# Moving the pads around h: the split activations 128 bytes instead of 64 off the weights' place in a 256-byte line

## The chip, the cores and the metric

The kernel runs on one core of a Trainium2 chip. The metric is the device time in microseconds (us), the median of the runs; lower is better. The core has TensorE (PE, matmuls; its weight loads are shown apart as PEld), VectorE (DVE), ScalarE (ACT), GpSimd (POOL), and SyncE (SP), which here only issues transfers (DMA).

## The reference

Two transformer blocks after one another, on 256 tokens of 1,024 values, all in float32. What is matrix work, in order (normalizations, modulation and residuals between them left out):

```python
# first block, layer 0
y = gmlp(h)                        # h @ w_in (1024 x 4096), spatial mix, @ w_out
x = x + g2 * moe(h)                # 64 experts, 8 for each token, 1 shared
# first block, layer 1
y = moba_attention(h)              # k, v, q, o projections of 1024 x 1024
x = x + g2 * moe(h)
# second block, layers l = 0 and 1
x = x + 0.5 * (silu(h @ Wg) * (h @ Wu)) @ Wd      # "ffn1": 1024 -> 2 x 2816 -> 1024
x = x + hybrid(h)                                 # h @ w_in (1024 x 5120), small mixes, @ w_out
x = x + 0.5 * (silu(h @ Wg) * (h @ Wu)) @ Wd      # "ffn2"
```

In each line `h` is the normalized `x`, newly made.

## The kernel before, in words

Tokens lie along the free dimension: `x` is a tile of 128 partitions by 8 groups of 256 tokens. The normalized activation is kept as two tiles of the same shape, `hH` (rounded to float32r) and `hL` (what the rounding left), and each weight in the same way as `WH` and `WL`. A product is then three matmuls, the function `mm3` at line 290: `WH` with `hH`, `WH` with `hL`, `WL` with `hH`. All go through `mm` at line 287, so the profile puts nearly every matmul down to L288.

Weights come in pieces of 1 MB (128 partitions by 2,048 float32) into a ring of nine slots, issued by SP. ACT rounds each piece into `WH` (L243), DVE makes `WL` (L246); there are two such pairs of buffers, so that a piece is split while another is used. A piece is an item; the items' order is written out by hand, and `run` at line 210 goes through it. The kinds of item that matter here:

- `proj_b` (line 381), the upward products of gmlp's second half, attention, hybrid and the feed-forward parts: weights from `WH`/`WL` stationary, 256 columns of `hH` or `hL` moving, 48 matmuls for each piece. `proj_a` (line 389) is the same with the sides changed: 128 columns of `hH` or `hL` stationary, 256 columns of `WH` or `WL` moving.
- `down_d` (line 396), the downward products: weights from `WH`/`WL` stationary, hidden values moving, which lie in the tile `rarena`; 48 matmuls for each piece. A feed-forward part is 22 upward and 11 downward items, mixed: two up, one down.
- `shared_mm` (line 1039), the shared expert: two of its upward steps take the stationary weights from `rarena` and move `hH` or `hL`.

At the start of each part of the second block the row of normalizers is made on TensorE: squares are summed (`stat_mm`, line 336), and two transposes (`stat_row`, L356, operands `cst` and `nv`) come between the third and the fourth item. The first of the feed-forward parts does this otherwise (`first_rows`, line 1534).

The tiles are laid out in a partition in the order of their declaration, each size rounded up to a multiple of 32 bytes. `WH`, `WL`, `x`, `hH`, `hL` are 16,384, 16,384, 8,192, 8,192 and 8,192 bytes, all multiples of 256, so that two tiles with no pad between them stand at the same place of a 256-byte line. With `pad0` of 64 bytes `hH` and `hL` stand 64 bytes behind the place of `WH` and `WL` in the line. With `pad1`, and the tiles after it, `rarena` too stands 64 bytes behind (it begins 107,584 bytes after `WH`, which is 420 lines and 64 bytes). All slices that matmuls take of these tiles are at multiples of 256 bytes from the tile's start, but for the scatter's and gather's small ones.

Of the kernel before, what the change touches and what calls it, by code (L numbers as in the profile page):

```python
# [8 lines left out]
F32 = mybir.dt.float32  # L9
# [85 lines left out]
def moba_moe_hybrid_kernel(ctx: ExitStack, tc: tile.TileContext, A: dict):  # L95
# [6 lines left out]
    def sb(shape, dt, name):  # L102
        return pool.tile(shape, dt, name=name)
# [5 lines left out]
    WL = sb([128, 4, 1024], F32R, "WL")  # L109
    x = sb([128, KD, T], F32, "x")  # L110

    sb([128, 16], F32, "pad0")
    hH = sb([128, KD, T], F32R, "hH")
    hL = sb([128, KD, T], F32R, "hL")
    sb([128, 16], F32, "pad1")
    cols = sb([128, NCOL], F32, "cols")
    cst = sb([128, NCST], F32, "cst")
    mbias = sb([128, 128], F32, "mbias")
# [1783 lines left out]
```

## Time and profile before

| | |
|---|---|
| time, median of 3 runs | 2583.36 us (2569.75, 2583.36, 2583.38) |
| profiled execution: time, span | 2581.31 us, 2579.3 us |
| PE, PEld | 95%, 73% of the span busy, 17,938 instructions each |
| DVE, ACT, POOL | 53%, 40%, 0% |
| DMA | 724 MB, mean 281 GB/s |
| granted TensorE clock, mean | 0.984 of full speed |

A matmul's record overlaps with the next one's: its busy time says when TensorE has something in it, not how fast it goes. The pace is the step from the start of one matmul to the start of the next.

### The profile page before, as it was taken

The numbers are of one execution on the slowest core, as the hardware profiler recorded it, in microseconds if no ns is written. First come the engines' busy times: TensorE is split into PE (matmuls) and PEld (weight loads), VectorE is DVE, ScalarE is ACT, GpSimd is POOL, SyncE is SP. The second block draws the span as 40 slices with busy tenths as digits, with TensorE's granted clock in tenths as the row PEclk, the third lists the DMA queues.
The fourth block names the chain that finished last, engine by engine and source line by source line (L and its number), as shares of the span: only waits on it lengthen the run. The fifth ranks groups of instructions, "written<-read, shape, count | busy, mean of one in ns | idle before, by whom it ended". The sixth has DMA issues, their size and how long they took to land. (4 is left out here: it accounts for less than half of the span.)

```text
span 2579.3 us, 43882 instructions
## 1 busy us (share of the span) xinstructions
PE 2437.8 (95%) x17938; PEld 1894.9 (73%) x17938; DVE 1359.6 (53%) x2536; ACT 1042.5 (40%) x1710; POOL 3.8 (0%) x6
## 2 busy tenths in 40 slices
PE   6998899999989979999999899999999999999998
PEld 4885554444448845544444699999999999999998
DVE  4556232332347643323233665788665666887665
ACT  3333222222225532212222444576544544684543
POOL 0000000000000000000000000000000000000000
PEclk9998999999999989999999899999999999999999
DMA  9878899999966389999999454354655553454750
GB/s 389 318 270 326 334 414 421 421 421 420 421 284 251 158 320 365 405 421 421 420 421 421 181 196 180 123 186 175 246 196 196 191 192 143 171 180 156 270 196 17
DMA packets 101437, 724.45 MB, mean 281 GB/s; under 512 B 11248, under 2 KB 12528, under 8 KB 14192
## 3 DMA queue, kind: packets, MB, share of 16 engines
q1 hardware_dynamic: 100080, 718.32, 70.7%
q8 instruction: 143, 2.34, 0.4%
q10 hardware_dynamic: 1152, 3.28, 0.3%
q14 instruction: 62, 0.51, 0.1%
HBM read 720.50 MB, written 1.05 MB: 280 GB/s over the span
## 5 line engine op out<-in xcount | busy, mean ns | idle before, releaser
L288 PE MATMUL pb<-rarena,WH 128*128 128x256 f32 x3552 | 701.5, 284 | 34.2 <-DVE farena L1207 22.0
L243 ACT CAST WH<-ring 128x1024 fp32r<-128x1024 f32 x476 | 489.4, 1047 | 434.2 <-PE pb L288 348.6
L288 PE MATMUL pb<-hH,WH 128*128 128x256 f32 x2336 | 654.1, 280 | 3.3 <-ACT hH L1505 2.4
L288 PE MATMUL pb<-hH,WL 128*128 128x256 f32 x2336 | 651.2, 279 | 2.5 <-DVE WL L246 2.4
L288 PE MATMUL pb<-hL,WH 128*128 128x256 f32 x2336 | 650.8, 279 | 0.0
L246 DVE TENSOR_TENSOR WL<-ring,WH 128x1024 fp32r<-128x1024 f32 x476 | 570.8, 1215 | 147.8 <-ACT WH L243 145.1
L288 PEld LDWEIGHTS pb<-rarena,WH 128*128 128x128 f32 x3552 | 577.0, 189 | 51.7 <-ACT farena L1110 28.2
L288 PE MATMUL pb<-rarena,WL 128*128 128x256 f32 x2224 | 591.8, 281 | 3.8 <-DVE WL L246 2.3
L288 PE MATMUL pb<-ring,farena 128*32 128x512 f32 (+2 forms) x2064 | 434.7, 595 | 23.4 <-DMA ring<-ex 23.4
L288 PEld LDWEIGHTS pb<-hH,WH 128*128 128x128 f32 x2336 | 440.1, 188 | 15.6 <-ACT WH L243 7.1
L288 PEld LDWEIGHTS pb<-hH,WL 128*128 128x128 f32 x2336 | 439.8, 188 | 3.9 <-DVE WL L246 3.7
L288 PEld LDWEIGHTS pb<-hL,WH 128*128 128x128 f32 x2336 | 440.0, 188 | 0.2 <-DVE hL L1502 0.2
L288 PEld LDWEIGHTS pb<-rarena,WL 128*128 128x128 f32 x2224 | 421.5, 190 | 5.7 <-DVE WL L246 3.0
L288 PEld LDWEIGHTS pb<-ring,farena 128*32 128x32 f32 (+2 forms) x2064 | 136.1, 130 | 239.9 <-issue 188.7
L1147 DVE SCALAR_TENSOR_TENSOR tmp<-pb,small,tmp 128x256 f32<-128x256 f32 x56 | 27.1, 484 | 413.0 <-ACT tmp L1145 413.0
L288 PE MATMUL pb<-ring,tmp 128*32 128x512 f32 (+2 forms) x1024 | 228.1, 605 | 16.8 <-DMA ring<-ex 8.6
L288 PEld LDWEIGHTS pb<-ring,tmp 128*32 128x32 f32 (+2 forms) x1024 | 70.0, 131 | 169.7 <-issue 145.7
L1180 DVE TENSOR_TENSOR WL<-pb,WH 128x512 fp32r<-128x512 f32 x112 | 77.5, 692 | 183.9 <-ACT WH L1179 183.9
L1207 DVE TENSOR_TENSOR farena<-farena,pb 128x512 f32<-128x512 f32 x208 | 133.6, 684 | 60.2 <-PE pb L288 60.2
L831 DVE TENSOR_TENSOR tmp<-pb,R 128x512 f32<-128x512 f32 x88 | 60.8, 691 | 184.8 <-PE pb L288 181.1
L1179 ACT CAST WH<-pb 128x512 fp32r<-128x512 f32 x112 | 65.7, 587 | 190.6 <-PE pb L288 190.6
L1161 ACT COPY tmp<-pb 128x256 f32<-128x256 f32 x56 | 20.9, 372 | 287.7 <-PE pb L1159 287.7
(301 smaller groups left out, 1710.6 us busy)
## 6 DMA issues: line engine op xcount, KB each, us to landing
ring<-ex SPq DMA_DIRECT2D x384, 1024.0 KB, 12.7
ring<-ada SPq DMA_DIRECT2D x56, 1024.0 KB, 8.3
ring<-f1u SPq DMA_DIRECT2D x44, 1024.0 KB, 4.8
ring<-f2u SPq DMA_DIRECT2D x44, 1024.0 KB, 4.9
ring<-win SPq DMA_DIRECT2D x40, 1024.0 KB, 4.8
ring<-f1d SPq DMA_DIRECT2D x22, 1024.0 KB, 4.8
ring<-f2d SPq DMA_DIRECT2D x22, 1024.0 KB, 4.8
ring<-lu SPq DMA_DIRECT2D x10, 1024.0 KB, 4.8
```

Source lines behind the costliest of these rows:

```text
L243: S.copy(hi, raw)
L246: V.tensor_sub(lo, raw, hi)
L288: P.matmul(out, l, r, start=start, stop=stop, skip_group_check=True, **kw)
L831: V.tensor_tensor(t.rearrange("p (a t) -> p a t", a=2), hold["p"].rearrange("p (a t) -> p a t", a=2), R.rearrange("p (o t) -> p o t", o=1) ...
L1147: V.scalar_tensor_tensor(hh, bank[:, 256:], wsl[:, b % 2:b % 2 + 1], t[:, :256], op0=ALU.mult, op1=ALU.mult)
L1161: S.copy(t, bank[:, :256])
L1179: S.copy(yH[:, fs], PB[DN[f]])
L1180: V.tensor_tensor(yL[:, fs], PB[DN[f]], yH[:, fs], op=ALU.subtract)
L1207: V.tensor_tensor(a2, a2, bank, op=ALU.add)
```

## The change

One pad of 128 bytes stands before `hH`, and none behind `hL`:

```diff
-    sb([128, 16], F32, "pad0")
+    sb([128, 32], F32, "pad0")
     hH = sb([128, KD, T], F32R, "hH")
     hL = sb([128, KD, T], F32R, "hL")
-    sb([128, 16], F32, "pad1")
     cols = sb([128, NCOL], F32, "cols")
```

`hH` and `hL` move up by 64 bytes; no other tile moves, since the two pads together were 128 bytes too. Against `WH` and `WL` they now stand 128 bytes off in the 256-byte line, against `rarena` 64 bytes (on the other side of the line's start), where they stood 64 and 0. No instruction is added, removed or moved.

## Rows read from the trace of the kernel before

**Rows 1.** Busy time by stage (--windows): length, engines' busy us (instructions), granted clock, DMA share, GB/s
```profile
0.00:160.00 160.00, 138.50 (x1082) 109.57 (x1083) 81.45 (x164) 62.41 (x91) 0.22 (x4) 0.97 0.86 339
445.00:770.00 325.00, 297.26 (x1668) 147.83 (x1667) 109.81 (x249) 74.40 (x153) 3.60 (x2) 0.99 0.96 398
900.00:1480.00 580.00, 528.03 (x3118) 289.34 (x3117) 208.97 (x520) 150.93 (x302) 0.00 (x0) 0.97 0.92 375
1480.00:1657.00 177.00, 176.96 (x1485) 176.24 (x1486) 110.14 (x157) 84.64 (x117) 0.00 (x0) 0.98 0.46 166
```

**Rows 2.** The page's costliest groups, those of matmuls with split operands
```profile
L288 PE MATMUL pb<-rarena,WH 128*128 128x256 f32 x3552 | 701.5, 284 | 34.2 <-DVE farena L1207 22.0
...
L288 PE MATMUL pb<-hH,WH 128*128 128x256 f32 x2336 | 654.1, 280 | 3.3 <-ACT hH L1505 2.4
L288 PE MATMUL pb<-hH,WL 128*128 128x256 f32 x2336 | 651.2, 279 | 2.5 <-DVE WL L246 2.4
L288 PE MATMUL pb<-hL,WH 128*128 128x256 f32 x2336 | 650.8, 279 | 0.0
```

**Rows 3.** The chain that ended last, long pieces: start us, us, what, instructions
```profile
1480.05 176.87 PE pb L288 x1482
...
1846.22 181.50 PE pb L288 x1604
2027.93 160.39 PE pb L288 x1415
...
2219.67 62.69 PE pb L288 x530
...
2335.87 63.98 PE pb L288 x547
...
2400.07 167.91 PE pb L288 x1480
```

**Rows 4.** Timeline of PE, shared expert: h moving, weights from rarena; start us, us, what
```profile
284.23 0.40 PE L288 MATMUL pb<-hH,rarena 128*128 128x256 f32 x2
...
284.95 0.40 PE L288 MATMUL pb<-hH,rarena 128*128 128x256 f32 x2
```

**Rows 5.** Timeline of PE: transposes at a part's start, and a wait
```profile
1845.84 0.38 PE L356 MATMUL pb<-cst,nv 128*128 128x128 f32 x2
...
2219.67 0.39 PE L288 MATMUL pb<-hH,WL 128*128 128x256 f32 x1 [0.27 <-DVE WL L246]
```

**Rows 6.** Timeline of PE in gmlp: weights moving and h stationary, then h moving
```profile
48.96 0.28 PE L288 MATMUL pb<-WH,hH 128*128 128x256 f32 x1
...
49.64 0.28 PE L288 MATMUL pb<-WH,hH 128*128 128x256 f32 x1
...
93.74 0.28 PE L288 MATMUL pb<-hH,WH 128*128 128x256 f32 x1
...
94.45 0.28 PE L288 MATMUL pb<-hH,WH 128*128 128x256 f32 x1
```

**Rows 7.** Work on hH alone by part of the second block (--windows): PE, PEld, DVE, ACT
```profile
1480.00:1657.00 177.00, 112.45 (x625) 96.28 (x625) 3.81 (x8) 3.98 (x8) 0.98 0.46 166
1657.00:1846.00 189.00, 114.63 (x641) 98.00 (x641) 3.81 (x8) 3.97 (x8) 1.00 0.52 190
1846.00:2019.00 173.00, 113.86 (x660) 99.96 (x659) 3.82 (x8) 3.98 (x8) 1.00 0.55 200
2019.00:2028.00 9.00, 8.80 (x48) 7.33 (x48) 0.00 (x0) 0.00 (x0) 1.00 0.62 237
2028.00:2194.00 166.00, 107.48 (x624) 94.45 (x623) 1.63 (x4) 1.99 (x5) 1.00 0.49 176
2194.00:2400.00 206.00, 129.56 (x721) 110.58 (x721) 6.05 (x13) 5.95 (x12) 1.00 0.50 185
2400.00:2573.00 173.00, 107.62 (x624) 94.37 (x623) 0.00 (x0) 0.00 (x0) 1.00 0.39 139
```

**Rows 8.** Timeline of PE in routing: sixteen float32 transposes in one run
```profile
901.83 1.91 PE L915 MATMUL pb<-cst,x 128*128 128x128 f32 x16
```

## The prediction

> **What bounds the kernel.** I read the stages first [rows 1]. From 0 to 160 us TensorE is busy for 138.5 of 160 us with transfers at 0.86. In the two expert stages (445 to 770 and 900 to 1480 us shown) the DMA share is 0.96 and 0.92, at 375 to 398 GB/s: the experts' weights set the time there. From 1480 us on it is TensorE's: busy for 176.96 of 177 us with transfers at 0.46. The chain that ended last agrees: its pieces there are long runs of L288 [rows 3]. So the last 1,100 us go as fast as one matmul follows another.
>
> The same rows give that pace. The feed-forward parts move the same shapes through the same lines, but 181.50 us for 1604 matmuls are 113.2 ns each, 160.39 for 1415 are 113.3, 167.91 for 1480 are 113.5, and the first part needs 176.87 for 1482, 119.3 (a few float32 sums among them); the second hybrid's pieces give 118.3 and 117.0. Taking out the sums, two paces stand there: a quick step of 113.3 ns and a slow one of 117.8 (six steps of 0.71 us at 93.74 are 118.3, read to 10 ns) [rows 3, 6]. The granted clock is 1.00 in both kinds of part [rows 7]. At both paces h moves against the split weights at a distance of 64 bytes; the step changes at events: slow until the two transposes at 1845.84, quick from the matmul after them through 181 us of up and down items; a wait of 0.27 us before 2219.67 opens a run of 62.69 us at 118.3 in the second hybrid [rows 3, 5], and the first hybrid runs alike. Within a run without a wait the pace is kept across up and down items, whose distance is the same 64 bytes. 13 of the run's 2581.31 us (2855 slow steps of h, below, by 4.45 ns) hang on which pace h is in; the three runs of the kernel differ by 13.6 us, which may be the same thing.
>
> **The change, part by part.** Nothing is added or removed; four things are read or written at another place.
>
> *h moving against WH and WL, distance 64 to 128 bytes.* No row shows a stream at 128. Rows at three other distances: 0 bytes (shared expert, `rarena` stationary), six steps in 0.72 us, 120 ns; +64, 113.3 or 117.8; −64 (weights moving, h stationary), six steps in 0.68 us, 113.3 [rows 3, 4, 6]. The two gmlp streams both begin after a short wait, and only the one at −64 is quick. So 0 is worst, ±64 are better, and on a circle of 256 bytes 128 is as far from 0 as one can be. If the pace at 128 mirrors that at 0 about the ±64 rows, it is 113.3 + 117.8 − 120 = 111.1 ns. That is an estimate from three points, and I don't trust the excess over the quick step. I take the quick step, 113.3, everywhere h moves against the split weights. Bounds: from below 109 ns, a far row: sixteen float32 transposes of 128 columns take 1.91 us, which less the 0.28 of one record is 15 steps of 109 [rows 8]; from above 120 ns, as at distance 0 [rows 4].
>
> How many steps: work on `hH` from 1480 us is 625 + 641 + 660 + 48 + 624 + 721 + 624 = 3943 matmuls, and `hL` has half as many [rows 2, 7], 5915 together. Slow are those of the first part (625 × 1.5 = 937), of the first hybrid less its three half-items after the transposes (641 × 1.5 − 73 = 888), 70 at 2019, and of the second hybrid less 121 in two short quick runs (721 × 1.5 − 121 = 960): 2855. The other 3060 are quick. Gain: 2855 × (117.8 − 113.3) = 12.7 us.
>
> *Down items behind them.* `rarena` doesn't move; its 528 matmuls in the first feed-forward part follow h without a wait and have kept h's pace so far. I let them turn quick with it: 528 × 4.45 = 2.3 us. Hybrid's own down items begin after waits of their own and stay as they are.
>
> *The stages before 1480 us.* gmlp's `proj_b` and attention's q and o move h in 384 matmuls each; all slow, that is 1.7 us each. TensorE is not always the bound there [rows 1], so I take 2 us of the 3.4. The shared expert's steps at distance 0 come to 64: 96 matmuls, 0.2 to 0.6 us, in a stage that the transfers bound: nothing, and 0.6 us if that cover were gone. `proj_a` goes from −64 to −128, the same place as +128: it is quick already, nothing; 384 × 6.7 = 2.6 us lost at 120.
>
> *Writes of h.* DVE and ACT write h at another place, eight times for each part, 3.81 and 3.98 us a part [rows 7]. Their shapes and counts stay; no row gives them a reason to change. They are on the chain at each part's start; a change by a tenth would be 0.4 us for each engine and part, under 5 us for six parts on both.
>
> *The bound next in line.* If TensorE gets quicker in the last 1,100 us, the transfers there are at 0.39 to 0.62 [rows 7] and don't become it.
>
> Sum: 12.7 + 2.3 + 2 = 17 us off 2581.31, 2564; off the median, which lies 2 us above the profiled run, **2566 us**. Its own range is 2558 to 2573, for the events that choose a pace need not fall as here.
>
> The Trainium skill speaks against any change: "SBUF — State Buffer", section "Who interferes with whom", gives TensorE two read ports, one for the moving operand and one for the weight load, independent of each other. By that the step would not hang on where h lies, and the time would stay. The rows of 120 ns at distance 0 speak against it as far as they go. "TensorE: Matmul & The Clock Gate", section "Back-to-back issue gap", gives 262 cycles for 256 columns, 109.2 ns at 2.4 GHz; by it even the quick step holds 4 ns of something else. No run here shows a split matmul at that step; with h undisturbed the time would be near that of rival 4.
>
> **The rivals.**
>
> 1. *Nothing but the events sets the pace* (0.22). The distance matters little, and ±64 and 128 share the two paces. For it: both paces occur at one and the same distance [rows 3]. Against it: the 120 ns. Time: 2583, with 10 us to either side for other parts in the quick step.
> 2. *The line that counts is 128 bytes long* (0.16), and 128 is the same as 0: slower. ±64 would then be one and the same place, the farthest from a collision, and it is true that the quick step occurs at both. Place: each matmul of h against the split weights. Price: quick steps 3060 × 6.7 = 20.4, slow ones 2855 × 2.2 = 6.3, the 1584 down matmuls of the three quick parts thrown into the slow step 7.0, and 2 us of the early stages and of `proj_a`: 36 less what is covered, say 30, 2613 us. It decides as soon as h's step lies over 115.5 ns, the mean of now (2855 at 117.8, 3060 at 113.3).
> 3. *The transposes no longer lead into the quick step* (0.10). At 128 the place in time at which they end fits otherwise, and every part stays slow: 3060 × 4.45 + 1584 × 4.45 = 20.7 us, 2604.
> 4. *h is undisturbed at 128* (0.14) and steps at the 109 ns of the transposes [rows 8]: 2855 × 8.8 + 3060 × 4.3 = 38 us, with 2.3 + 3 around it 43: 2540. Against it: no split product at any distance comes under 113.3 in the rows.
>
> **How the numbers follow.** The forecast has 0.38. Faster by over 0.5%, which is about what a measurement of this kernel tells from no change, is under 2570.4; slower is over 2596.3. Faster: four fifths of the forecast, rival 4, a quarter of rival 1: 0.30 + 0.14 + 0.05 = 0.49, which I round down to 0.47, since the estimate at 128 rests on three points. Slower: rivals 2 and 3, and a little of 1: 0.28. The same: 0.25. The range from 2538 to 2608 holds the forecast, rivals 1, 3 and most of 4, and a part of 2: some 8 in 10.
>
> **What would show it.** The chain's pieces from 1480 us: the first feed-forward part at 1482 matmuls should take near 168 us instead of 176.87, hybrid's first run of 530 near 60 instead of 62.69, and the three quick parts should stay at 113.3. Right is the forecast if up items step at 113.3 even after a wait; the down items show whether the pace is carried over at a change of distance. Wrong it is if up and down items of one part step differently, up slower (rival 2), or if the part after 1846 us is slow throughout (rival 3). Counts, groups and transfers must stay as they are.

## The result, and the profile after

The change made the kernel slower: 2599.34 us, median of five runs (2598.6 to 2608.09), against 2583.36 us, median of five of the kernel before (2569.75 to 2583.42). The ratio is 1.0089, 95% interval 1.0062 to 1.0116. In a second comparison (after2, below) it was 1.0112 (1.0088 to 1.0135; 2605.57 against 2577.3). The profiled execution took 2606.1 us with a span of 2604.0, which is 24.7 us over the span before.

With one line less above it, `mm` is now line 287 of the program. First the page of the kernel after: its span, the engines' busy time, and the groups that answer to [rows 2].

```profile
span 2604.0 us, 43882 instructions
...
PE 2463.4 (95%) x17938; PEld 1922.8 (74%) x17938; DVE 1359.6 (52%) x2536; ACT 1041.7 (40%) x1710; POOL 3.8 (0%) x6
...
L287 PE MATMUL pb<-rarena,WH 128*128 128x256 f32 x3552 | 709.6, 285 | 34.2 <-DVE farena L1206 22.1
...
L287 PE MATMUL pb<-hH,WH 128*128 128x256 f32 x2336 | 661.7, 283 | 3.1 <-ACT hH L1504 2.4
L287 PE MATMUL pb<-hH,WL 128*128 128x256 f32 x2336 | 659.2, 282 | 1.6 <-DVE WL L245 1.6
```

The counts are those of before. Busy time rose where a split operand moves: the two groups of `hH` by 7.6 and 8.0 us, and that of `rarena` by 8.1 us, although `rarena` stays at its place. The waits at the ends of these lines are the old ones to within 1 us. So TensorE does the same work at another pace. The chain tells where (start us, us, what, instructions):

```profile
1482.62 176.46 PE pb L287 x1482
...
1848.58 189.15 PE pb L287 x1604
2037.94 167.50 PE pb L287 x1415
...
2353.23 64.09 PE pb L287 x547
...
2417.53 175.26 PE pb L287 x1480
```

Beside [rows 3], the three pieces that had been quick are longer by 7.65, 7.11 and 7.35 us, 22.1 together. The second block starts 2.57 us later. The first feed-forward part is 0.4 us shorter, and each hybrid as a whole is longer by 0.2 to 0.3 us. Nothing else of size is left of the 24.7.

The first feed-forward part can't be compared by its length alone, because TensorE's clock differs there. Its first 7 us before, after and in a later run, all112 (--windows: length, PE, PEld, DVE, ACT, POOL, granted clock, DMA share, GB/s):

```profile
1480.05:1487.05 7.00, 7.00 (x36) 7.00 (x37) 6.49 (x10) 4.39 (x7) 0.00 (x0) 0.56 0.41 152
...
1482.62:1489.62 7.00, 7.00 (x46) 7.00 (x47) 6.49 (x10) 4.40 (x7) 0.00 (x0) 0.76 0.41 152
...
1476.78:1483.78 7.00, 7.00 (x61) 7.00 (x62) 6.49 (x10) 4.88 (x8) 0.00 (x0) 1.00 0.42 152
```

In the same time TensorE got through 36, 46 and 61 matmuls. The kernel after spent less of this stretch at the lower of the two clock levels (1.2 against 2.4 GHz) than the kernel before and won 10 matmuls, over 1 us; that hides the 0.8 us by which the 933 steps of h there grew (117.8 to 118.7).

The pace itself is read from the starts of single matmuls. TensorE's timeline of the kernel after, right behind the two transposes in which the quick run had begun [rows 5], and further on where a down item follows (start us, us, what):

```profile
1848.19 0.38 PE L355 MATMUL pb<-cst,nv 128*128 128x128 f32 x2
...
1848.77 0.28 PE L287 MATMUL pb<-hH,WH 128*128 128x256 f32 x1
...
1849.84 0.28 PE L287 MATMUL pb<-hH,WH 128*128 128x256 f32 x1
...
1856.96 0.40 PE L287 MATMUL pb<-rarena,WH 128*128 128x256 f32 x2
...
1858.72 0.40 PE L287 MATMUL pb<-rarena,WH 128*128 128x256 f32 x2
```

The first two `hH` rows are nine steps apart: 1.07 us, 118.9 ns each. The two `rarena` rows are fifteen steps apart: 1.76 us, 117.3 ns. Read in this way over the second block, h steps at 118.7 ns everywhere and the down items at 117.8. Before, from 1480 us on, 3047 steps of h were quick (113.3) and 2838 slow (117.8), and 1584 down steps were quick and 1688 slow. In the three parts that had been quick this comes to about 2853 × 5.35 = 15.3 us for h and 1584 × 4.45 = 7.0 us for the down items, 22.3 us together, against the 22.1 that the chain shows.

### The profile page after: what moved, and what is told of

Same layout as the page of the kernel before. It is cut to its first block, busy times and chain, and to the rows that moved or that the text cites. A ratio compares the mean times of both kernels' runs of the same rounds, so it can differ in the third digit from the quotient of the medians.

```text
span 2604.0 us, 43882 instructions
## 1 busy us (share of the span) xinstructions
PE 2463.4 (95%) x17938; PEld 1922.8 (74%) x17938; DVE 1359.6 (52%) x2536; ACT 1041.7 (40%) x1710; POOL 3.8 (0%) x6
## 4 chain that ended last, share of the span: by engine, by line
PE 60%; DVE 4%; DMA 4%; ACT 3%; issue 1%; SPq 0%; DVEq 0%; ACTq 0%
PE pb L287 59%; DMA ring<-ex 3%; DVE WL L245 1%; ACT WH L242 1%; DVE farena L1206 1%; ACT rarena L297 0%; DMA ring<-f1u 0%; DVE rarena L298 0%; DVE tmp L1738 0%; DVE x L1245 0%; PE pb L1158 0%; PE pb L1122 0%; DVE tmp L1731 0%; PE pb L1414 0%; ACT ring L1698 0%
## 5 line engine op out<-in xcount | busy, mean ns | idle before, releaser
L287 PE MATMUL pb<-rarena,WH 128*128 128x256 f32 x3552 | 709.6, 285 | 34.2 <-DVE farena L1206 22.1
L287 PE MATMUL pb<-hH,WH 128*128 128x256 f32 x2336 | 661.7, 283 | 3.1 <-ACT hH L1504 2.4
L287 PE MATMUL pb<-hH,WL 128*128 128x256 f32 x2336 | 659.2, 282 | 1.6 <-DVE WL L245 1.6
L287 PE MATMUL pb<-hL,WH 128*128 128x256 f32 x2336 | 658.7, 282 | 0.1
L287 PEld LDWEIGHTS pb<-hH,WH 128*128 128x128 f32 x2336 | 441.0, 189 | 15.3 <-ACT WH L242 6.7
## 6 DMA issues: line engine op xcount, KB each, us to landing
ring<-ex SPq DMA_DIRECT2D x384, 1024.0 KB, 12.7
```

What stands on the lines that cost most here:

```text
L287: P.matmul(out, l, r, start=start, stop=stop, skip_group_check=True, **kw)
```

## The experiments

The theories: *distance* (h's step is a function of its place against the weights, modulo some line; rival 2 and the forecast are both of this kind), *events* (rival 1: waits and transposes alone choose the pace) and *carry-over* (the pace of one stream passes to the next). All runs but the two scans are the whole kernel. Steps and counts are worked out from the starts of matmuls in each trace, counted from 1480 us on.

**scan: one stream at sixteen distances.** This kernel leaves the reference's computation out. It runs streams of 48 matmuls with slices of `WH` stationary and a tile moving that stands 0, 16, ... 240 bytes off in the line, each three times after a wait and three times right behind two transposes; at the end the sides are changed for four distances.

```python
for rep, n in enumerate((256, 128, 192)):
    for d in DIST:          # 0, 16, ... 240
        wait(p, d, n)
        stream(d)
        turn()              # two transposes
        p = stream(d)
```

> The kernel leaves out the whole computation and writes x: it only times streams of 48 float32r matmuls of 256 columns, stationary from one tile, moving from a tile that stands 0, 16, ... 240 bytes behind it in a 256-byte line, three times each after a short wait and three times straight after two transposes. Theory 1 (the step hangs on the distance in a 256-byte line): 120 ns at 0, 118.7 at 128, and at 64 and 192 either 113.3 or 117.8, with the values between them changing steadily or by steps; the streams with sides changed behave like the mirrored distance. Theory 2 (a line of 128 bytes): each distance has the same step as the one 128 bytes on, so 0 equals 128 and 64 equals 192. Theory 3 (the distance has no part, only what stands ahead of the stream): the same set of steps at all distances.

TensorE's timeline of the scan, with tile `ata` at 0 bytes, `ate` at 64, `atg` at 96, `ath` at 112, `ati` at 128 (start us, us, what, matmuls, and in brackets the wait before):

```profile
22.44 6.01 PE L56 MATMUL pb<-ata,WH 128*128 128x256 f32 x48 [0.77 <-ACT ata L65]
...
79.02 5.90 PE L56 MATMUL pb<-ate,WH 128*128 128x256 f32 x48
...
98.39 6.01 PE L56 MATMUL pb<-atg,WH 128*128 128x256 f32 x48 [0.82 <-ACT atg L65]
...
111.21 5.76 PE L56 MATMUL pb<-ath,WH 128*128 128x256 f32 x48 [0.82 <-ACT ath L65]
...
116.94 5.74 PE L56 MATMUL pb<-ath,WH 128*128 128x256 f32 x48
...
123.50 5.96 PE L56 MATMUL pb<-ati,WH 128*128 128x256 f32 x48 [0.82 <-ACT ati L65]
...
129.44 5.94 PE L56 MATMUL pb<-ati,WH 128*128 128x256 f32 x48
...
640.40 5.71 PE L56 MATMUL pb<-WH,ate 128*128 128x256 f32 x48 [0.82 <-ACT ate L65]
```

A row is 48 matmuls: the first one's delay, the steps and the last record. The step, the mean from the starts inside without the first few, is in ns, and repetitions agree within 0.2:

| bytes | 0 | 16 | 32 | 48 | 64 | 80 | 96 | 112 |
|---|---|---|---|---|---|---|---|---|
| step | 120.0 | 118.6 | 116.7 | 118.3 | 117.8 | 118.3 | 120.0 | 113.9 |
| **bytes** | **128** | **144** | **160** | **176** | **192** | **208** | **224** | **240** |
| step | 118.65 | 118.7 | 118.7 | 119.2 | 117.8 | 119.2 | 118.3 | 117.1 |

So here distance sets the pace, against *events*: the same 48 matmuls behind the same wait take 5.76 us at 112 bytes and 6.01 at 96. 118.65 at 128 is what the changed kernel shows. The function is not smooth: 112 is a single dip between 120.0 and 118.65; its streams begin with a dozen steps of 114 to 121 ns and then go at 113.3, and 113.9 is the mean of both. 112 and 240 differ by 3.2 ns and 0 and 128 by 1.35, so the line isn't 128 bytes. With the sides changed, 64 gives 113.3. The scan's fifteen streams at 64 with the weights stationary were never quick, two transposes ahead of them or not; so transposes alone don't bring about the quick step that the kernel before shows.

**h0: h at distance 0, `rarena` still at 64.**

```diff
-    sb([128, 16], F32, "pad0")
     ...
-    sb([128, 16], F32, "pad1")
+    sb([128, 32], F32, "pad1")
```

> h at 0, rarena left at 64 (pads of 0 and 128). Theory 1: h steps at 120 ns everywhere in the second block, down items at 117.8 throughout: 3060 x 6.7 + 2855 x 2.2 + 1584 x 4.45 = 34 us over before, 2615. Theory 2: as the changed kernel, 118.7 ns, 2599 to 2608. Theory 3: as before.

2617.03 us in a single run, against a median of 2577.41 for the kernel before on the same chip. h stepped at 120.0 throughout, and no down step was quick; the part of 1604 matmuls took 190.59 us. That is what distance gives: 1.3 ns a step dearer than 128 bytes, as in the scan.

**h192: h at 192, `rarena` at 64.** Both pads were made 192 bytes.

```diff
-    sb([128, 16], F32, "pad0")
+    sb([128, 48], F32, "pad0")
     ...
-    sb([128, 16], F32, "pad1")
+    sb([128, 48], F32, "pad1")
```

> h at 192 bytes (64 before the weights' place in the line), rarena left at 64, by pads of 192 and 192. Theory 1 (distance in 256 bytes): h at -64 can step at 113.3; if it goes there after waits too, as the streams at -64 in gmlp did, all of its 5,900 steps of the second block are quick and the time is near 2566 to 2570, and the down items show whether the quick step is carried from -64 to +64. Theory 2 (128 bytes): the same as before, 2570 to 2584. Theory 3: the same as before.

2579.11 us (2573.16 to 2588.46), ratio 1.0013 (0.9995 to 1.0032): no difference. Inside it there are two that cancel: 5035 steps of h were quick and 848 slow, more than before, while of the down items only 112 were quick and 3180 slow, behind a quick h and without a wait between. So here the pace doesn't carry over from h to `rarena` when their distances differ.

**shift: the changed kernel, 128 bytes further on.** A pad ahead of the ring of weights moves everything, and leaves all distances as in the changed kernel (the edit is shown against the kernel before).

```diff
+    sb([128, 32], F32, "padr")
     ...
-    sb([128, 16], F32, "pad0")
+    sb([128, 32], F32, "pad0")
     ...
-    sb([128, 16], F32, "pad1")
```

> The changed kernel with everything 128 bytes further up: all distances as in the changed kernel, every tile on the other half of its 256-byte line. If the distance between h and the weights counts, h steps at 118.7 ns and the time is 2598 to 2608. If the place of h itself counts (it goes from 0 to 128 in the line), the step changes; the weights then stand at 0 and rarena at 64.

2592.96 us in a single run. Not one step of h was quick, and the pieces of 1604, 1415 and 1480 matmuls took 189.15, 167.50 and 175.26 us, to 0.01 us those of the kernel after. So for h distance counts, not its own place. The time lies 13 us under that of the kernel after's profile: 8.6 us of it before the second block starts, which a single run doesn't explain; 1.5 in the first feed-forward part (174.94 us; its first 7 us had a granted clock of 1.00, against 0.76); and 3.1 in the two hybrids' last down pieces (62.54 and 62.53 us for 547 matmuls). There, 729 of the down items' 3,250 steps were quick, against 3 in the kernel after, with every distance the same: at 64 bytes distance alone does not fix the pace.

**scan2: a finer scan, 0 to 504 bytes by 8.** As the first, computation left out, each distance once after a wait and once behind transposes.

> The computation is left out as in the first scan. Moving tiles at 0, 8, ... 504 bytes behind the weights, and at 100, 108, 116 and 124, each timed once after a wait and once after two transposes. Theory 1 (distance in a line of 256 bytes): the step at a distance and at that distance plus 256 is the same; the multiples of 16 repeat the first scan (120.0 at 0, 113.9 at 112, 118.7 at 128). Rival (the line is 512 bytes or longer): the second half differs from the first, and may hold distances that neither scan nor kernel has used.

Timeline of TensorE in the second scan: `aao` at 112, `abu` at 368, `abb` at 216, `ach` at 472 bytes.

```profile
223.13 5.76 PE L56 MATMUL pb<-aao,WH 128*128 128x256 f32 x48 [0.82 <-ACT aao L65]
...
388.38 6.17 PE L56 MATMUL pb<-abb,WH 128*128 128x256 f32 x48 [0.82 <-ACT abb L65]
...
630.98 5.76 PE L56 MATMUL pb<-abu,WH 128*128 128x256 f32 x48 [0.82 <-ACT abu L65]
...
796.24 6.17 PE L56 MATMUL pb<-ach,WH 128*128 128x256 f32 x48 [0.82 <-ACT ach L65]
```

Distances 256 bytes apart give the same row, but for 8 and 264 and for 16 and 272, which differ in which of two steps they take. The steps go from 113.3 (192 and 448) to 123.4 ns (216 and 472), and odd multiples of 8 are mostly at 120 or more. No stream's step came under 113.3.

Several distances have two steps. 192 gave 113.3 here and 117.8 in the first scan. At 8, 32, 80, 144, 168, 200 and 232 bytes the stream behind the transposes stepped 1.0 to 3.4 ns otherwise than the one after a wait, to either side; at 144 (tile `aas`) it is 118.7 after the wait and 116.6 behind them:

```profile
273.92 5.96 PE L56 MATMUL pb<-aas,WH 128*128 128x256 f32 x48 [0.82 <-ACT aas L65]
...
279.85 5.85 PE L56 MATMUL pb<-aas,WH 128*128 128x256 f32 x48
```

So what runs ahead of a stream has a part too, at some distances.

**all192: h and `rarena` both at 192.** Only `pad0` grows, to 192 bytes; `rarena` and all tiles between follow.

> h and rarena both at 192 bytes (pads of 192 and 64). If the pace is kept across items only where their distance is the same, and at 192 most starts lead into the quick step (as h alone did, 5035 of 5883 steps), then up and down items of the second block are nearly all quick: against before, 1975 h steps and 1688 down steps gain 4.45 ns each, 16 us: near 2561 to 2567. If 192 is no different from 64: as before, 2567 to 2584.

2590.18 us (2580.66 to 2597.81), ratio 1.0052 (1.0037 to 1.0067). I had expected 2561 to 2567, and that fell: h was quick in 895 steps and slow in 4989, down items in 906 and 2390. In h192 h stood at the same distance and was quick in 5035. At 192, as at 64, one distance has two paces, and which one comes hangs on something else, such as what ran before or where the tiles behind h stand.

**r128: h unmoved at 64, `rarena` to 128.** The pad behind `hL` also moves the tiles between it and `rarena` by 64 bytes, the transposes' operands `cst` and `nv` among them.

```diff
-    sb([128, 16], F32, "pad1")
+    sb([128, 32], F32, "pad1")
```

> h stays at 64 as before, rarena alone moves to 128 (pads of 64 and 128). If the quick step is lost whenever a stream at another distance comes between, h is quick only from the transposes to the first down item (some 150 matmuls of each part) and slow after it, though nothing of h has changed; down items step at 118.7: 2,900 h steps lose 4.45 ns, 1584 down steps 5.3 and 1688 0.9: 23 us, 2600 to 2607. If each stream has its own pace, h is as before and only the down items lose 10 us: 2590.

2604.71 us in a single run. The chain's long pieces of this kernel, where of the two streams only the down items were moved:

```profile
1848.61 188.65 PE pb L288 x1604
2037.47 167.07 PE pb L288 x1415
...
2416.64 174.85 PE pb L288 x1480
```

The down items step at 118.7, and h, which was not moved, lost the quick step too: 141 quick steps of some 5,900. It was slow also right behind the transposes, nine steps in 1.06 us:

```profile
1848.23 0.38 PE L356 MATMUL pb<-cst,nv 128*128 128x128 f32 x2
...
1848.80 0.28 PE L288 MATMUL pb<-hH,WH 128*128 128x256 f32 x1
...
1849.86 0.28 PE L288 MATMUL pb<-hH,WH 128*128 128x256 f32 x1
```

The time came as expected; but I had expected h to stay quick up to the first down item, and it did not. So in these runs the quick step at 64 hardly comes about when h and `rarena` stand at different distances (in the hybrids' down pieces of shift a part of it did), and setting either of them to 128 costs about the same. Whether it is `rarena`'s place that took h's quick step, or that of a tile which moved with it, no run separates; the same holds for all192.

**all112: h and `rarena` both at 112, the scan's dip.** The tiles' sizes are rounded to 32 bytes, so the last 16 come from slices that begin four values into a larger tile.

```diff
-    sb([128, 16], F32, "pad0")
-    hH = sb([128, KD, T], F32R, "hH")
-    hL = sb([128, KD, T], F32R, "hL")
-    sb([128, 16], F32, "pad1")
+    sb([128, 24], F32, "pad0")
+    hh = sb([128, 2 * KD * T + 8], F32R, "hh")
+    hH, hL = [hh[:, 4 + i * KD * T:4 + (i + 1) * KD * T].rearrange("p (k t) -> p k t", k=KD) for i in range(2)]
+    sb([128, 8], F32, "pad1")
     ...
-    rarena = sb([128, RW], F32R, "rarena")
+    rarena = sb([128, RW + 8], F32R, "rarena")
     ...
-        return rarena[:, off:off + n]
+        return rarena[:, 4 + off:4 + off + n]
```

> h and rarena both at 112 bytes, the one distance of the scan with a quick step however the stream begins (113.8 to 114.0 ns). Theory 1: all 5,915 h and 3,272 down steps of the second block at 113.9: the slow ones gain 3.9 ns (4,540, 17.7 us), the quick ones lose 0.5 (4,640, 2.5 us): 15 us under before's usual 2583, near 2566 to 2569, and with less spread between runs. Theory 3 (distance has no part): as before.

2563.22 us (2562.69 to 2566.01), ratio 0.9947 (0.993 to 0.9965): faster than both kernels. Its chain:

```profile
1476.78 167.76 PE pb L288 x1482
...
1831.18 181.33 PE pb L288 x1604
2012.73 160.43 PE pb L288 x1415
...
2319.79 61.86 PE pb L288 x547
...
2381.88 167.95 PE pb L288 x1480
```

The first feed-forward part is 9.1 us shorter than before and at the pace of the three others, which keep theirs; each hybrid's last long piece gains 2.1 us. Of h's and the down items' steps 8829 are quick and 322 slow. Against the 4631 quick ones of before that is 4198 × 4.45 = 18.7 us; the spans differ by 18.3 (2579.3 to 2561.0). That the two agree is chance. From the second block's start on, the gain is 15.0 us; the other 3.3 lie before it. Of the 9.1 us of the first feed-forward part, some 1,430 steps account for 6.4, and the rest is the clock (36 and 61 matmuls in the first 7 us, above). The two hybrids gain 2.7 and 3.0 us, where their newly quick steps would give some 6 each: there a quicker TensorE waits more for the low halves of the weights. TensorE's waits in the first hybrid, before and in all112 (us, times, longest):

```profile
PE pb L288 <- DVE WL L246: 1.1, 2, 0.8
...
PE pb L288 <- DVE WL L246: 3.2, 6, 1.0
```

**h112: h at 112, `rarena` at 64.** The edit of all112 for `hh` alone, without a second pad, so that `rarena` keeps 64.

> h at 112 bytes, rarena left at 64. Theory 1 with each stream's pace its own and a changed distance breaking the hand-over: h at 113.3 to 113.9 nearly everywhere (2855 slow steps gain 4 to 4.45 ns, 12 us), down items at 64 behind it slow as behind h at 192 (1584 steps lose 4.45, 7 us): 4 to 6 us under before, a ratio of 0.998. If down items go on with h's pace: 17 us and more, as at 112 for both, 0.994.

2576.62 us (2574.19 to 2582.15), ratio 1.0001 (0.999 to 1.0011). TensorE's timeline where a down item follows h with no wait:

```profile
1875.78 0.39 PE L287 MATMUL pb<-hh,WH 128*128 128x256 f32 x2
...
1877.14 0.39 PE L287 MATMUL pb<-hh,WH 128*128 128x256 f32 x2
...
1877.48 0.40 PE L287 MATMUL pb<-rarena,WH 128*128 128x256 f32 x2
...
1879.25 0.40 PE L287 MATMUL pb<-rarena,WH 128*128 128x256 f32 x2
```

Twelve steps of h in 1.36 us are 113.3 ns, and from the very next matmul fifteen steps of `rarena` in 1.77 us are 118.0. Over the trace h was quick in 5659 steps and slow in 224, the down items quick in 4 and slow in 3278. By the counts that is (5659 − 3047) × 4.45 = 11.6 us won and 1580 × 4.45 = 7.0 lost; the interval allows 2.6 of the 4.6 us that should remain. The profile shows where the count fails: the three feed-forward parts that had been quick lose 2.1 to 2.4 us each, as counted, but the hybrids gain only 1.0 and 1.4 us, where h's newly quick steps would give 3.6 and 3.8. The first part gains 6.8, of which 4.0 are h's steps and the rest again the clock.

**h128r112: the changed kernel with `rarena` at 112.**

```diff
+    sb([128, 8], F32, "pad1")
     ...
-    rarena = sb([128, RW], F32R, "rarena")
+    rarena = sb([128, RW + 8], F32R, "rarena")
     ...
-        return rarena[:, off:off + n]
+        return rarena[:, 4 + off:4 + off + n]
```

> The changed kernel with rarena at 112 instead of 64. If the down items' loss in the changed kernel comes of their distance of 64 behind a stream of another one, they are quick here (3,272 steps at 113.3 to 113.9, 13 to 14 us under the changed kernel) while h stays at 118.7. If a slow h stream makes any down stream behind it slow, the time is that of the changed kernel.

2593.92 us (2592.02 to 2595.3), ratio 1.0064 (1.0043 to 1.0085). h stays at 118.7, and the down items are quick in 2712 steps and slow in 588, mostly the first dozen behind h, as in the scan's streams at 112.

**after2: the changed kernel again, beside it.**

> The changed kernel once more, beside the other two on one chip. Every theory: h at 118.7 ns throughout, down items at 117.8, a ratio to before of 1.006 to 1.012.

2605.57 us (2603.21 to 2609.52), with pieces of 189.15, 167.50 and 175.25 us. h128r112 is 11.7 us quicker, and 2712 × 4.45 = 12.1. In the three later feed-forward parts the count fits: 1206 quick down steps × 4.45 = 5.4 us, and the pieces are 1.86, 1.62 and 1.85 shorter, 5.3 together. The first part is 3.4 shorter, about 1.6 of it by the clock, and the hybrids 3.6, where the count gives 4.8. So the 7.0 us that the change took from the down items are got back without moving h; the rest is gained on down steps that were slow before the change too.

## Why the prediction was wrong

What bounds the kernel was read rightly. Nearly all the difference that can be placed is TensorE's step; transfers, counts, waits and the writes of h stayed as forecast. In the feed-forward parts the price of one step (4.45 ns between the two paces) comes out to 0.1 us (h128r112).

**The step that failed is "I take the quick step, 113.3, everywhere h moves against the split weights".** It rested on an estimate of 111.1 ns from three distances and a mirror on a circle of 256 bytes. The circle is right (the second scan), the mirror is not: 118.65 ns at 128 in the scan and 118.7 in the kernel, with 113.9 at 112 bytes beside it. Three points couldn't show that; 118.7 lay inside the bounds of 109 and 120 that the step named, but not at the end that I took. In place of 12.7 us won on the slow steps, the quick ones lost 15.3 us.

**The second step that failed is "I let them turn quick with it".** The pace isn't carried from one distance to another. h112 and h192 have slow down items right behind a quick h, all112 has both quick at one distance. In the changed kernel, where h and `rarena` stand apart, the 1584 down steps that had been quick lost 7.0 us, where 2.3 us of gain were forecast. In r128, the other way round, it is h that is slow, with the doubt named there.

**The early stages** were forecast to gain 2 us, with "it is quick already, nothing" for `proj_a`. That failed too. TensorE's timeline of the kernel after in gmlp, beside [rows 6]:

```profile
48.84 0.28 PE L287 MATMUL pb<-WH,hH 128*128 128x256 f32 x1
...
49.91 0.28 PE L287 MATMUL pb<-WH,hH 128*128 128x256 f32 x1
```

Nine steps in 1.07 us: over all of `proj_a` the step rose from 113.5 to 118.7 ns, 2.0 us for 384 matmuls, and that of the early products that move h from 117.4 to 118.7, 1.4 us for some 1,090. The second block began 2.57 us later, but how much of that is these steps isn't shown: after2 began it at 1482.90 us, and shift, with the same steps, at 1473.98.

**Two sizes were wrong besides.** 8.2 of the 12.7 us (888 and 960 steps) were to be won in the hybrids at the full price of a step; all112, which did bring the quick step there, won about half of what its count gives. And "the granted clock is 1.00 in both kinds of part" passes over the 0.98 that [rows 7] have for the first part: part of its 119.3 ns a matmul was the clock, which is why it went to near 168 us in all112, while the forecast's own steps bring it to 170.3 only.

The rivals:

- *Only events set the pace* falls by the scan and h0. What is left of it is that 64 and 192 have two paces each, and that in the second scan the step at some other distances hung on whether a wait or transposes came before.
- *A line of 128 bytes* falls as a mechanism (0 and 128 differ by 1.35 ns, 112 and 240 by 3.2). Its break-even holds: h's mean step rose over 115.5 ns, to 118.7, and the time went to that side. Its price was 30 us, because it took 120.
- *The transposes no longer lead into the quick step* came nearest in size, 20.7 us forecast and 22.1 in the three parts. But at 128 there is no quick step for them to lead into: none of the first scan's seven streams at 128 is quick, three of them right behind transposes.
- *h undisturbed at 109 ns* never occurred. 113.3 ns, which is 272 cycles of 2.4 GHz at the granted clock of 1.00 [rows 7], is the least of all distances. The Trainium skill's 262 cycles ("TensorE: Matmul & The Clock Gate", "Back-to-back issue gap"), which the section gives for a single matmul by itself, were reached by no split stream here.

With little changed but the distance, the step of these float32r streams goes from 113.3 to 123.4 ns (second scan). That refutes what the prediction drew from the Trainium skill's two independent read ports ("SBUF — State Buffer", "Who interferes with whom"), that the step would not hang on where h lies; whether it is the ports that are not independent, no run here shows.

Open is what selects between 113.3 and 117.8 at 64 and 192 bytes. Two transposes don't suffice (scan, r128), a neighbour at the same distance doesn't either (all192), and with all distances kept the share of quick down steps went from almost none to a fifth (shift). That the two operands' reads collide is my picture of it; the traces show steps, and no reads.

## What to carry to other kernels

Where TensorE sets the end and each matmul brings its own weights, the place of the moving operand against the stationary one in the 256-byte line is worth up to 9% of the step (113.3 to 123.4 ns in the scans); measure it with a scan of all distances, since it can't be worked out from a few. Choose a distance whose stream is quick however it begins, and put all streams that alternate there (112 bytes here, 0.5% of the whole kernel): at 192, quick in one scan and slow in the other, the whole kernel lost, and moving h alone to 112 left the time as it was, for the down items lost about what h won. Count the gain only where TensorE's step sets the time; in the hybrids of all112 about half of it was lost again, mostly in waits. And when a pad moves a tile, list which other distances it changes: here the loss at the tile that stood still was a third of the whole.

## What was unexpected of the hardware

The dip at 112 bytes, 113.9 ns between 120.0 at 96 and 118.65 at 128, and its absence at 240 (117.1). That the sides matter: at 64 bytes the tile `ate` moving stepped at 117.8 in all of the first scan's streams, the weights moving at 113.3 (by distance that is 192 bytes, where the second scan has 113.3 too and the first 117.8). And that one stream's pace can hang on tiles that it doesn't touch: in r128 h was slow in almost all of its steps, though only `rarena` and the tiles between had been moved.
